# A row softmax on one core: the first load issued ahead of the entry barrier

## Chip, cores and metric

One NeuronCore of one Trainium2 chip. The metric is the device time of one execution in microseconds (us), as the median of a few runs.

## The reference

```python
x: (16, 1024, 512) float32
x_max = max(x, axis=-1)
exp_x = exp(x - x_max)
out   = exp_x / sum(exp_x, axis=-1)
```

It reads 33.55 MB and writes 33.55 MB.

## The kernel before

The 16384 rows are cut into 16 tiles of 128 partitions x 8 rows x 512 (2 MB each). Loads are issued by SyncE, stores by ScalarE. VectorE takes the row maxima and does the scaling, ScalarE the exponentials and their sums. The tiles have twelve buffers, and the loads run far ahead of the stores: in the packet records of this kernel the last load packet ends at 131.6 us, the last store packet at 160.17.

```python
CHUNKS = [8] * 16
SLOTS = {8: 12}
# ... pools, views src[k] and dst[k] ...
    def load(k):
        R = CHUNKS[k]
        tiles[k] = data.tile([P, R, d], F32, name=f"x{R}", tag=f"x{R}", bufs=SLOTS[R])
        nc.sync.dma_start(out=tiles[k], in_=src[k])
    # ... rowmax(k): one VectorE reduction of 128x4096
    # ... exps(k): 8 ScalarE activations with row sums
    # ... scale(k): one reciprocal and 8 multiplications on VectorE
    def store(k):
        nc.scalar.dma_start(out=dst[k], in_=tiles[k])

    with tc.manual_schedule():
        for k in range(K):
            load(k)
            rowmax(k)
            exps(k)
            if k >= 1:
                scale(k - 1)
                store(k - 1)
        scale(K - 1)
        store(K - 1)
```

What the source does not show is the program's first block, which the framework writes ahead of this code. Its instructions stand in the trace. GpSimd fills four small constants by memset, from 0.24 to 0.44 us. Then all five engines pass a barrier, a point that none leaves before all have reached it, kept by semaphores (counters that engines raise and wait for): each of the other four drains and adds one to a semaphore, between 0.01 and 0.34 us; GpSimd drains from 0.30 to 0.49, looks at that semaphore at 0.53, and at 0.61 releases them through a second one; they go on at 0.65 to 0.66. All code above stands behind that barrier, the first load too, which is issued at 0.73.

## Time and profile before

Time before: 163.15 us (162.96 to 163.39, 3 runs), span of the profiled run 161.3 us.

| what | us | where to read it |
|---|---|---|
| work of the 16 DMA engines | 158.2 of 161.3 | queue table: 49.5% + 48.6% of the span |
| VectorE busy | 123.8 | busy table |
| ScalarE busy | 93.2 | busy table |
| SyncE held by the entry barrier | 0.7 | waits of SyncE's queue |
| first load's issue starts | 0.73 | timeline |

The page's DMA lines of the kernel before follow; a packet is one of the pieces in which a DMA moves its data, of 16 KB in this kernel. The first two lines have 40 equal slices of the span, about 4 us each: the busy share of the DMA engines in tenths, and GB/s moved.

```profile
DMA  6999999999999999999999999999999999999993
GB/s 163 431 427 427 431 435 378 418 445 431 423 439 431 421 435 431 431 439 418 439 435 427 431 427 435 435 425 435 431 427 439 431 427 427 431 435 431 431 435 171
...
q1 hardware_dynamic: 2304, 33.56, 49.5%
q10 hardware_dynamic: 2304, 33.56, 48.6%
```

The reader should see a stream that is full from the second slice to the last but one. Queue 1 carries the loads and queue 10 the stores. Only the first and the last slice are short (163 and 171 GB/s; the others have 378 to 445), and from the first packet's start at 1.74 us to the last one's end at 160.17 there are 158.4 us for 158.2 us of work. So a change elsewhere can hardly win anything; time is to be had at the two ends alone.

Now the start. In the timeline (start, duration, engine; "SPq" is SyncE's queue issuing DMAs, merged over several issues) of the kernel before:

```profile
0.24 0.10 POOL L110 MEMSET const-float32-0.0<- 128x1 f32 x1 [0.24 <-issue]
...
0.33 0.10 POOL L110 MEMSET const-uint8-127<- 128x1 uint8 x1
0.73 8.22 SPq L52 DMA_DIRECT2D x<-in_x_dram  x7
8.64 4.42 DVE L57 TENSOR_REDUCE shift<-x 128x8 f32<-128x4096 f32 x1 [8.64 <-DMA x<-in_x_dram]
```

And in the waits of SyncE's queue (total us, times, longest), the line of the entry barrier:

```profile
SPq L110 <- PEq L110: 0.7, 1, 0.7
```

Nothing is loaded until SyncE is through the barrier, at 0.73 us, and nothing is computed until the first tile has landed, at 8.64 us. The wait line names PE, because TensorE was the last engine to add to the semaphore. But the records of the single instructions show that GpSimd was the last at the barrier: SyncE arrives at 0.00 us, VectorE and ScalarE at 0.13, TensorE at 0.32, and GpSimd looks at the count at 0.53, after its memsets and its drain, and releases at 0.61.

### The profile page before, as it was taken

What the parts mean: (1) busy time and instruction counts of PE and PEld (TensorE: products, weight loads), DVE (VectorE), ACT (ScalarE), POOL (GpSimd) and SP (SyncE); (2) the same over time, 40 slices, a digit from 0 to 9 for tenths busy, and PEclk for the clock granted to TensorE, in tenths of its full rate; (3) what the DMA queues carried; (4) which work ended last, traced back from release to release, by engine and by line L of the source; (5) the groups of instructions that cost most, each with busy time, mean ns of one, the idle gap of its engine ahead of it and who ended that gap; (6) DMA issues with size and microseconds to landing.
All of it is one profiled execution on the core that took longest, in us unless ns stands there. A gap on an engine that the chain in (4) does not pass through costs nothing.

```text
span 161.3 us, 527 instructions
## 1 busy us (share of the span) xinstructions
DVE 123.8 (77%) x160; ACT 93.2 (58%) x257; POOL 0.2 (0%) x4
## 2 busy tenths in 40 slices
DVE  0088799999999999985970079999999999957000
ACT  0037994959596867067002996859595959591000
POOL 0000000000000000000000000000000000000000
DMA  6999999999999999999999999999999999999993
GB/s 163 431 427 427 431 435 378 418 445 431 423 439 431 421 435 431 431 439 418 439 435 427 431 427 435 435 425 435 431 427 439 431 427 427 431 435 431 431 435 171
DMA packets 4612, 67.14 MB, mean 416 GB/s; under 512 B 513, under 2 KB 513, under 8 KB 513
## 3 DMA queue, kind: packets, MB, share of 16 engines
q1 hardware_dynamic: 2304, 33.56, 49.5%
q10 hardware_dynamic: 2304, 33.56, 48.6%
q14 instruction: 4, 0.02, 0.0%
HBM read 33.55 MB, written 33.55 MB: 416 GB/s over the span
## 4 chain that ended last, share of the span: by engine, by line
DMA 52%; DVE 31%; ACT 6%; SPq 2%; issue 1%; ACTq 1%; DVEq 0%
DMA x<-in_x_dram 52%; DVE shift L57 16%; DVE x L77 14%; ACT x L63 6%; SPq L52 2%; DVE recip L75 1%; ACTq L84 0%; DVEq L121 0%; ACTq L63 0%
## 5 line engine op out<-in xcount | busy, mean ns | idle before, releaser
L63 ACT ACTIVATE x<-x,shift 128x512 f32<-128x512 f32 x128 | 90.5, 709 | 44.1 <-DVE shift L57 21.4
L57 DVE TENSOR_REDUCE shift<-x 128x8 f32<-128x4096 f32 x16 | 70.6, 4415 | 9.7 <-DMA x<-in_x_dram 9.7
L77 DVE TENSOR_SCALAR x<-x,recip 128x512 f32<-128x512 f32 x128 | 52.1, 482 | 0.6
L63 ACT ACTIVATION_READ_ACCUMULATOR x<-x,shift 128x1 f32 x128 | 24.0, 187 | 0.0
L75 DVE RECIPROCAL recip<-sums 128x8 f32<-128x8 f32 x16 | 3.1, 196 | 15.3 <-ACT x L63 15.3
L63 ACT ACT_TABLE_LOAD x1 | 1.3, 1283 | 8.7 <-DMA x<-in_x_dram 8.7
L110 POOL MEMSET const-bfloat16-1.0<- 128x1 bf16 x1 | 0.1, 102 | 0.0
L110 POOL MEMSET const-uint8-127<- 128x1 uint8 x1 | 0.1, 102 | 0.0
L110 POOL MEMSET const-float32-0.0<- 128x1 f32 x1 | 0.1, 99 | 0.2 <-issue 0.2
L110 POOL MEMSET const-float32-1.0<- 128x1 f32 x1 | 0.1, 99 | 0.0
## 6 DMA issues: line engine op xcount, KB each, us to landing
x<-in_x_dram SPq DMA_DIRECT2D x16, 2048.0 KB, 42.6
out_dram<-x ACTq DMA_DIRECT2D x16, 2048.0 KB, 18.0
```

The lines of the kernel that those rows point to most:

```text
L52: nc.sync.dma_start(out=tiles[k], in_=src[k])
L57: nc.vector.reduce_max(out=shift[k], in_=tiles[k], axis=AX, negate=True)
L63: nc.scalar.activation(out=tiles[k][:, r, :], in_=tiles[k][:, r, :], func=EXP, bias=shift[k][:, r : r + 1], scale=1.0, accum_out=sums[k][: ...
L75: nc.vector.reciprocal(out=recip, in_=sums[k])
L77: nc.vector.tensor_scalar_mul(out=tiles[k][:, r, :], in0=tiles[k][:, r, :], scalar1=recip[:, r : r + 1],)
L110: nc = _bacc.Bacc("TRN2", target_bir_lowering=False, num_devices=1)
```

## The change

The intent: SyncE reaches the barrier first and idles there, from 0.00 to 0.65 us. The first load waits for nothing, since its buffer is fresh and its input is there, so it can be issued in that idle time. The edit works on the finished program: it takes the first DMA out of the kernel's block and puts it ahead of SyncE's drain in the first block.

```diff
+def first_load_at_the_head(nc):
+    main, body = nc.main_func.blocks[0], nc.main_func.blocks[1]
+    dmas = [i for i in body.instructions if type(i).__name__ == "InstDMACopy"]
+    load = dmas[0]
+    assert load.engine == mybir.EngineType.SP
+    body.instructions.remove(load)
+    barrier = next(
+        n
+        for n, i in enumerate(main.instructions)
+        if i.engine == mybir.EngineType.SP and type(i).__name__ == "InstDrain"
+    )
+    main.instructions.insert(barrier, load)
 # ...
     nc = tc.nc
+    nc.at_finalize(first_load_at_the_head)
```

## The prediction

> **What bounds it now.** The 16 DMA engines. The queue table gives loads 49.5% and stores 48.6% of their span: 98.1% of 161.3 us, or 158.2 us. In the slices DMA stands at 9 tenths in 38 of 40, near 430 GB/s; only the first (163 GB/s) and the last (171) are short. [...] In the packet records the first load packet starts at 1.74 us and the last store packet ends at 160.17: a window of 158.4 us for 158.2 us of work, so time can only be won at its two ends. The timeline has VectorE and ScalarE done at 149.5 us.
>
> **The start (instruction records).** SyncE reaches the barrier first, at 0.00 us. VectorE and ScalarE come at 0.13 to 0.14, TensorE at 0.32; GpSimd is last: its four memsets (0.24 to 0.44) and its drain (0.18 us) let it see all four at 0.53 and release at 0.61. SyncE is released at 0.65 and issues the first load at 0.73. The wait view of SyncE's queue shows the same: 0.7 us, once. First packet 1.01 us after the issue began, 0.64 after it ended; tile complete at 8.63.
>
> **What the change does.** It adds and removes no instruction and no byte. It moves one issue of 0.37 us ahead of SyncE's barrier wait, into idle time. Order on other engines is unchanged.
>
> - Gain: the first issue at about 0.00 instead of 0.73, the first packet at about 1.0.
> - Kept later? The second load issues right after the barrier, at 0.75 to 0.85 (1.15 before). The first 2 MB need 4.9 us at 430 GB/s, so the engines never run out. The whole stream should move up.
> - Cost: SyncE arrives at about 0.40 and drains. A drain does not wait for the data: ScalarE's after the last store's issue took 0.15 us while that store ran for 10 us more. So SyncE is through at about 0.57, near the 0.53 at which GpSimd looks; the barrier may slip 0.05 to 0.1 us. Nothing critical waits for it: later loads have 4 us of slack, the engines wait for data until about 8 us.
>
> **Critical path.** All of the 0.73 us, since the first load heads the DMA stream and the first reduction. I take 0.7, allowing for an issue slightly after SyncE's arrival. That is 0.4%. Measured time is 1.8 us over the span; I take that as fixed.
>
> **Predicted:** 163.15 - 0.7 = 162.45 us; 162.0 to 162.9 eight times in ten. Faster by over 2%: 0.01; within 2%: 0.97; slower by over 2%: 0.02.
>
> **What would show it.** First load issued near 0 us; second at 0.75 to 0.85; first packet near 1.0; first reduction at about 7.9 instead of 8.64; first slice up from 163 to about 240 GB/s (0.73 us at 430 is 0.31 MB, my estimate); span 160.6; DMA work still about 158 us; last compute 0.7 us earlier.
>
> **What would make it wrong.** SyncE's drain waiting for the load to land: every engine held to about 8 us, the DMA engines dry for about 2 us between loads one and two, and the time up by 1 to 3 us. A slow first issue so early, or something in the launch that holds its packets. A span that starts with SyncE, whose arrival need not be tied to the measured start of the run. The two streams meeting in another phase[...].

Two passages of this text are cut where marked: a sentence that set the rate of the full slices beside a figure from outside this case, and the size put on the last risk, which no run showed. The 430 GB/s used in the text is read from the GB/s line above.

## The result

| | median us | range | runs | span of the profiled run |
|---|---|---|---|---|
| before | 163.17 | 162.96 to 163.39 | 4 | 161.3 |
| after | 162.39 | 162.29 to 162.55 | 4 | 160.6 |

The ratio is 0.9953, with a 95% interval of 0.9936 to 0.997. Here and below a ratio is the mean time of one kernel's runs over that of the other's runs of the same rounds, so it is not quite the ratio of the medians quoted. The kernel is 0.78 us faster, well inside the 2% that counts as the same, yet clear of noise.

The DMA lines of the page after:

```profile
DMA  7999999999999999999999999999999999999993
GB/s 233 441 424 428 441 420 371 437 430 428 428 433 433 430 424 437 437 420 437 424 437 441 420 432 428 433 439 420 428 433 432 441 428 424 433 433 437 424 433 167
...
q1 hardware_dynamic: 2304, 33.56, 49.7%
q10 hardware_dynamic: 2304, 33.56, 48.8%
```

Only the first slice has clearly changed, from 163 to 233 GB/s; the others differ by at most 19 GB/s, either way. The shares have risen because the span is shorter: 98.5% of 160.6 us is 158.2 us of work, as before.

The timeline and the barrier's wait line after:

```profile
0.00 8.04 SPq L68 DMA_DIRECT2D x<-in_x_dram  x7
0.23 0.10 POOL L126 MEMSET const-float32-0.0<- 128x1 f32 x1 [0.23 <-issue]
...
0.33 0.10 POOL L126 MEMSET const-uint8-127<- 128x1 uint8 x1
7.72 4.42 DVE L73 TENSOR_REDUCE shift<-x 128x8 f32<-128x4096 f32 x1 [7.72 <-DMA x<-in_x_dram]
```

```profile
SPq L126 <- PEq L126: 0.2, 1, 0.2
```

The issue starts at 0.00, the first reduction 0.92 us earlier. The barrier itself opens a little later: GpSimd releases at 0.654 instead of 0.608 us, because SyncE's drain after the issue takes 0.13 us and ends at 0.55. The second load is issued at 0.78 us (1.15 before), and nothing else that waits at the barrier is needed so soon: the first reduction starts at 7.72.

To see whether the lead is kept I sorted the end times of all 4096 data packets (16 KB each) of each trace. This is a reading of the raw packet records:

| packet, in order of its end | before, us | after minus before, us |
|---|---|---|
| 16th | 3.76 | -0.78 |
| 128th | 8.04 | -0.78 |
| 512th | 22.62 | -0.78 |
| 1025th | 42.70 | -0.75 |
| 1537th | 62.15 | -0.64 |
| 3073rd | 120.56 | -0.66 |
| last | 160.17 | -0.69 |

The whole stream is moved, by the 0.73 us that the issue has moved, give or take 0.1.

### The profile page after: what moved, and what is told of

Same layout as the page of the kernel before. It is cut to its first block, busy times and chain, and to the rows that moved or that the text cites. A ratio compares the mean times of both kernels' runs of the same rounds, so it can differ in the third digit from the quotient of the medians. Undisturbed runs are those within 1.5% of the kernel's fastest.

```text
span 160.6 us, 527 instructions
## 1 busy us (share of the span) xinstructions
DVE 123.8 (77%) x160; ACT 93.2 (58%) x257; POOL 0.2 (0%) x4
## 4 chain that ended last, share of the span: by engine, by line
DMA 52%; DVE 31%; ACT 7%; SPq 1%; issue 1%; ACTq 0%; DVEq 0%
DMA x<-in_x_dram 52%; DVE shift L73 16%; DVE x L93 14%; ACT x L79 7%; SPq L68 1%; DVE recip L91 1%; ACTq L100 0%; DVEq L137 0%; ACTq L79 0%
```

## The experiments

The theory: the time is the moment at which the DMA stream starts, plus a fixed length, as long as the engines never run dry; the change moves that start. Rivals: the gain comes from compute starting earlier; or from the barrier or the later loads having moved; or the start is covered by slack and the gain has another source. All results were correct against the reference. "Before" is the kernel before on the same chip, in the same rounds. The changed kernel was not run again there: where a run is set against its 162.39 us, the two are of different rounds, in which the kernel before agrees (163.10 to 163.19, against 163.17).

| run | us (range) | before | ratio, 95% interval |
|---|---|---|---|
| 1: before, barrier 3.9 us later | 167.02 (166.91 to 167.24) | 163.13 | 1.0238, 1.0224 to 1.0251 |
| 2: after, barrier 3.9 us later | 163.64 (163.10 to 164.53) | 163.13 | 1.0032, 1.0009 to 1.0054 |
| 3: after, barrier 10 us later | 168.14 (168.07 to 168.36) | 163.13 | 1.0307, 1.0293 to 1.032 |
| 4: six loads ahead, barrier 10 us later | 162.29 (162.26 to 162.41) | 163.13 | 0.9948, 0.9936 to 0.996 |
| 5: two loads ahead, barrier 3.9 us later | 162.37 (162.18 to 162.47) | 163.10 | 0.9952, 0.9939 to 0.9964 |
| 6: one load ahead, barrier 1.9 us later | 162.43 (162.25 to 162.49) | 163.10 | 0.9954, 0.9941 to 0.9966 |
| 7: second load ahead instead of the first | 162.21 (162.16 to 162.48) | 163.10 | 0.9948, 0.9936 to 0.9961 |
| 8: first load in 64-partition halves, two queues | 168.03 (167.52 to 168.46) | 163.10 | 1.0293, 1.027 to 1.0316 |
| 9: first load in row halves, two queues | 162.41 (162.27 to 162.63) | 163.19 | 0.9954, 0.994 to 0.9967 |
| 10: 64-partition halves, one queue | 166.64 (166.46 to 166.84) | 163.19 | 1.0212, 1.0198 to 1.0226 |
| 11: row halves, one queue | 162.48 (162.42 to 162.74) | 163.19 | 0.9961, 0.9949 to 0.9974 |
| 12: before, without the four memsets | 155.00 (154.55 to 155.06) | 163.19 | 0.9493, 0.948 to 0.9506; not comparable, see 12 |

### 1. The barrier is made late, and the load stands behind it

GpSimd gets extra memsets of a scratch tile, moved into the first block ahead of its drain. They are about 1.0 us apart.

```diff
+    scratch = data.tile([P, PAD], F32, name="scratch", tag="scratch", bufs=1)   # PAD = 1024
     with tc.manual_schedule():
+        for _ in range(NPAD):                                                   # NPAD = 4
+            nc.gpsimd.memset(scratch, 0.0)
+    # on the finished program: these NPAD memsets to GpSimd's end of the barrier
```

> The kernel before, with four extra GpSimd memsets of 128x1024 ahead of the barrier, so that SyncE is released d later than 0.65 us (d is read from the trace; I guess 3 to 5 us). The first load still stands behind the barrier. Theory (the time hangs on when the first load is issued, and the DMA engines are full from then on): time = before + d, all of it, because the stream starts d later and nothing can be caught up. Rival (the start is hidden by slack somewhere later, and the 0.7 us of the change came from something else): clearly less than d is lost, down to nothing.

The timeline of this run:

```profile
0.37 3.98 POOL L118 MEMSET scratch<- 128x1024 f32 x4
4.66 3.15 SPq L81 DMA_DIRECT2D x<-in_x_dram  x6
```

The issue starts at 4.66 instead of 0.73 us, 3.93 later, and the time rises by 167.02 - 163.13 = 3.89 us. A delay of the first issue is paid in full and nowhere caught up. The rival with slack somewhere later falls.

### 2. The same late barrier, with the load ahead of it

```diff
+    # as in 1, NPAD = 4, and the first load to SyncE's end of the barrier
```

> The changed kernel with the same four extra memsets. Theory: the first load is issued at 0.0 us all the same, its 2 MB keep the DMA engines busy until about 7 us, the second load needs about 1 us from issue to first packet, so any barrier that opens before about 6 us costs nothing: time within 0.3 us of the changed kernel (162.4), although all engines are held d longer. If the barrier opens at 6 to 7 us, up to 1 us is lost. Rival (the change helped by opening the barrier or the rest of the program earlier): time = changed + d.

The time is 163.64 us: of the 3.9 us of delay, 1.25 us are lost against 162.39, and the runs scatter over 1.4 us. This was a miss for my "within 0.3 us". The load ahead of the barrier saves most of the 3.9 us, though not all, so the rival "changed + d" (166.3) falls too. The windows of 1 us around the place where the first load runs out (the last two columns are the DMA share and GB/s) show this, here the changed kernel:

```profile
7.00:8.00 1.00, 0.28 (x1) 0.23 (x1) 0.00 (x0) 1.00 1.07 459
8.00:9.00 1.00, 1.00 (x1) 1.00 (x1) 0.00 (x0) 1.00 0.99 426
```

and here this run:

```profile
7.00:8.00 1.00, 0.12 (x1) 0.07 (x1) 0.00 (x0) 1.00 0.92 328
8.00:9.00 1.00, 1.00 (x1) 1.00 (x1) 0.00 (x0) 1.00 0.85 360
```

Between 7 and 9 us the stream is short of its 430 GB/s. In the packet records the packets that end there took 0.70 and 0.66 us on average, up to 1.0, instead of 0.61. Runs 5 and 6 below ask whether the late second load is the reason.

### 3. A barrier so late that the first load is used up

```diff
+    # as in 2, NPAD = 10
```

> The changed kernel with ten extra memsets: the barrier opens at r (about 8 to 12 us), when the first load has been consumed. Theory: the engines run dry from about 7.3 us until r + 1.1 us (second load's issue to first packet), so time = 162.4 + (r + 1.1 - 7.3), give or take 0.6 us for ramps; the packet records show one gap of that length. Rival (only the first load's place matters): 162.4.

SyncE is released at 10.62 us, so the expectation was 162.4 + (10.62 + 1.1 - 7.3) = 166.8, give or take 0.6. Measured: 168.14. The direction is right, but the size is 1.3 us short, outside the margin of 0.6. The windows show why:

```profile
6.00:7.00 1.00, 0.00 (x0) 0.00 (x0) 0.94 (x2) 1.00 0.65 279
7.00:8.00 1.00, 0.00 (x0) 0.00 (x0) 0.94 (x2) 1.00 0.04 16
8.00:9.00 1.00, 0.00 (x0) 0.00 (x0) 0.94 (x2) 1.00 0.00 0
...
11.00:12.00 1.00, 1.00 (x1) 1.00 (x1) 0.00 (x0) 1.00 1.08 213
12.00:13.00 1.00, 1.00 (x1) 0.05 (x1) 0.00 (x0) 1.00 0.45 131
13.00:14.00 1.00, 1.00 (x1) 0.00 (x0) 0.00 (x0) 1.00 0.86 360
```

The engines do run dry: the first load's last packets end between 6.8 and 7.7 us, and the next packet starts at 11.66. (A packet's bytes and time are shown where it starts, so 11 to 12 us shows packets that had only begun.) Then they need until about 14 us to be back at rate: the first sixteen packets again take 0.6 to 1.8 us each, most of them over 1 us, as at the program's start (0.95 to 1.86 us in the kernel before, where later ones take 0.61). My sum left out this second ramp (the time that a starting stream needs to come to its full rate). From the packet records, the 256th packet is 5.65 us later than in the changed kernel: 4.4 us of this are the gap of my sum, the rest is the ramp.

### 4. The same very late barrier, six loads ahead of it

```diff
+    # NPAD = 10, and the first six loads to SyncE's end of the barrier
```

> As the run with ten memsets, but with all six loads that wait for nothing placed ahead of the barrier (12 MB, 29 us of stream). Theory: the DMA engines never run dry, and compute, which starts at r instead of 7.7 us, has some 10 us of slack at the end, so the time is back within 0.5 us of 162.4. Rival (the loss of the ten-memset run is the late compute, not the dry engines): as slow as that run.

162.29 us: everything is back. Two lines of its timeline:

```profile
2.71 10.25 SPq L81 DMA_DIRECT2D x<-in_x_dram  x3
10.74 4.42 DVE L86 TENSOR_REDUCE shift<-x 128x8 f32<-128x4096 f32 x1 [10.74 <-PEq L142]
```

The first reduction starts at 10.74 us, just as late as in run 3, and is held by the barrier; the time does not care. What run 3 lost was the dry stream, not the late compute.

### 5 and 6. Why run 2 lost 1.25 us

```diff
+    # 5: NPAD = 4, two loads ahead of the barrier
+    # 6: NPAD = 2, one load ahead of the barrier
```

> The four-memset run took 163.64 us, 1.25 more than I expected, with a wide spread (163.1 to 164.5). Theory A (partly dry engines): the second load, issued at 4.66 us, reached the engines too late to be queued behind the first load's last packets, which shows as packets of 0.7 us mean instead of 0.61 between 7 and 9 us. Here the same four memsets stand ahead of the barrier, but two loads stand ahead of it too. A: back at 162.4, within 0.25, spread back to 0.3 us. Theory B (the memsets themselves, or the late barrier, cost it): as slow as that run, 163.6.

> One load ahead of the barrier, two extra memsets, so the barrier opens at about 2.6 us and the second load is issued at about 2.7, 4 us before the first load's last packets. Theory A: 162.4, within 0.25, although the barrier is 2 us later than in the changed kernel. Theory B: about half of the loss of the four-memset run, 163.0.

162.37 and 162.43 us, both with the small spread back. Run 5 has the same memsets and the same late barrier as run 2, so neither of these cost anything. Its windows at the place where run 2 fell short:

```profile
7.00:8.00 1.00, 0.28 (x1) 0.24 (x1) 0.00 (x0) 1.00 0.96 410
8.00:9.00 1.00, 1.00 (x1) 1.00 (x1) 0.00 (x0) 1.00 1.07 459
```

With the second load issued at 2.64 us (run 6) nothing is lost; at 4.66 (run 2) 1.25 us are. So the latest harmless issue of the second load lies somewhere between 2.6 and 4.7 us, although the first load's last packets end only around 7 us. Run 6 also rules out that the change won its time by issuing the second load earlier (0.78 us against 1.15 before): here it is issued later than before, and the time is the changed kernel's. In the packet records run 2 is 0.48 us behind the changed kernel at the 256th packet, 0.8 at the 769th, about where the stores begin, and 1.07 at the last.

The order of packet ends hides one thing that the landing marks of the same two traces show. Each DMA leaves 16 marks as its parts land. For the second load their mean is only 0.37 us later in run 2, but the last of them comes at 14.00 us instead of 12.59, and 0.96 us after the one before it. The third and fourth loads show the same gap and again end 1.4 us late (18.90 against 17.48, 23.80 against 22.37), and the last mark of the last store is 1.09 us late (160.90 against 159.81). So in this one trace the loss is there from the second load on, at first chiefly in one part of sixteen, and compute starts only after the last mark (the first reduction at 7.88 us, the first load's last mark at 7.85). By the last store the mean of the marks is 0.82 us late too. The marks do not tell which engine the slow part belongs to. Why it fell behind, how the lag spread, and why the loss scatters from run to run, is open.

### 7. The second load ahead of the barrier instead of the first

```diff
-    # dmas[0] is moved
+    # dmas[1] is moved: tile 1 lands first, tile 0 after it
```

> The second load, not the first, is placed ahead of the barrier; the first stays behind it. The stream starts at the same time as in the changed kernel, but tile 0 lands about 5 us later, so the first reduction starts at about 12.6 us instead of 7.7. Theory (what counts is when the DMA stream starts): 162.4, within 0.3. Rival (what counts is when the first tile is ready for compute): no gain over the kernel before, rather a loss of some 4 us (167).

The timeline of this run:

```profile
12.63 4.42 DVE L84 TENSOR_REDUCE shift<-x 128x8 f32<-128x4096 f32 x1 [12.63 <-DMA x<-in_x_dram]
```

The first reduction starts 4.9 us later than in the changed kernel and even 4 us later than before, and the time is 162.21 us, the changed kernel's within noise. So the earlier compute that the change brings is worth nothing here. What counts is when the stream starts, with any load.

### 8 to 11. Can the ramp be shortened as well?

In the changed kernel the first packet starts at 1.02 us and the 16th ends at 2.99; at full rate the 16 engines would have a packet each by 1.63 (an estimate: 1.02 plus the 0.61 us of a steady packet). I tried to shorten this by having two queues issue halves of the first load.

```diff
-        nc.sync.dma_start(out=tiles[k], in_=src[k])
+        if k == 0:                        # 8
+            h = P // 2
+            nc.sync.dma_start(out=tiles[k][:h], in_=src[k][:h])
+            nc.scalar.dma_start(out=tiles[k][h:], in_=src[k][h:])
+        else:
+            nc.sync.dma_start(out=tiles[k], in_=src[k])
+    # 9: halves [:, :h] and [:, h:] with h = R // 2; 10: as 8, both by sync; 11: as 9, both by sync
+    # in all four both halves go ahead of the barrier
```

> The first load is cut in two halves of 64 partitions, one issued by SyncE and one by ScalarE, both ahead of the barrier[...]. In the changed kernel the first packet starts at 1.02 us and the 16th ends at 2.98 (a full-rate start would have it end at 1.63). If the issue time of 0.37 us is part of that ramp, the 64th packet ends 0.1 to 0.25 us earlier than in the changed kernel and the time is 162.15 to 162.3[...]. Half the chance each.

> The first load cut in two again, one half by SyncE and one by ScalarE ahead of the barrier, but each half of all 128 partitions (4 of their 8 rows, packets of 8 KB). The run with 64-partition halves took 5 us more (I had expected 0 to 0.25 less): its packets took 1.29 us instead of 0.61. Theory S[...]: here no such packets, time 162.2 to 162.6. Theory Q (two queues at once in the first microseconds disturb each other): several us slower, 165 or more. The first question stays too: is the 64th packet's worth of bytes (1.05 MB) earlier than in the changed kernel (4.82 us)?

> Both 64-partition halves issued by SyncE, one after the other, ahead of the barrier. Theory S: the halves run at about 200 GB/s one after the other, some 5 us lost: 167 to 168.5, packets of 1.2 to 1.3 us until about 11 us. Theory Q: full rate, 162.4.

> The control of the two-queue run by rows: the same two halves of 128 partitions, both issued by SyncE ahead of the barrier. Packets of 8 KB. Time 162.4 within 0.25; if the smaller first packets shorten the ramp, 1 MB is in before 4.82 us and the time is 162.2. The difference to the two-queue run is the second queue's alone.

Three clauses are cut from these texts, since no run shows the mechanisms that they name: one from run 8's reason for two queues, one from its other case (no gain, 162.4 us, which had the other half of the chance), and the reason given for theory S. Theory S, and what runs 9 and 10 test, is that the cut by partitions makes the packets slow. Its about 200 GB/s in run 10's text are an estimate from run 8: a packet of 16384 bytes in 1.29 us on each of 16 engines makes 203.

Run 8 was a bad miss: 168.03 us. Its two possible causes, the 64 partitions and the second queue, are told apart by 9 and 10. With two queues but all 128 partitions (9) nothing is lost; with one queue and 64 partitions (10) 3.5 us are lost against before. The start of run 10's GB/s line:

```profile
GB/s 191 191 254 429 401 441 445 425 401 443 445 429 421 421 443 441 425 413 437 445 433 417 421 445 437 429 415 433 441 441 429 413 433 441 437 417 421 445 441 147
```

In the second slice the halves move at 191 GB/s, under half of the 441 that the 128-partition loads reach in that slice of the changed kernel. Run 11, with the same one queue and two halves but all 128 partitions, takes 162.48 us, so it is the cut by partitions that costs; why it does was not shown. I had not thought of it when I cut the load that way. Run 8 lost 1.4 us more than run 10: its second half, issued by ScalarE at 0.12 us, had its first packet only at 5.9 us (in run 9, issued at the same time, at 2.80). Why it was held is open.

The ramp question itself: in runs 9 and 11, with packets of 8 KB, the first 1.05 MB are in at 4.41 and 4.46 us instead of 4.86, and the first 8.4 MB at 21.70 and 21.68 instead of 21.89. But 33 MB are in at 79.72 and 79.83 instead of 79.63. I take a part of the early lead to be only that small packets are counted as done sooner, which no run shows; the 0.2 us that is left is gone again after the stores have begun. With 162.41 and 162.48 us there is no gain, and two queues do no better than one. The ramp stays, and what makes it was not shown.

### 12. A shorter barrier in the kernel before

```diff
+    # the kernel before; the four InstMemset of the first block are removed (nothing reads them)
```

> The kernel before, first load behind the barrier, with GpSimd's four unused constant memsets removed, so that GpSimd is no longer late. TensorE then comes last (0.32 us), so the first load's issue should move from 0.73 to 0.55 to 0.65 us, and the time by the same 0.1 to 0.2 us: 162.95 to 163.05 if before is 163.1; the stream's lead in the packet records is the same 0.1 to 0.2. If the barrier's length is not what the change hid, no such lead.

The measured time is 155.00 us (154.55 to 155.06), which looks like 8.2 us won. It is not. The head of the page and the timeline of this run:

```profile
span 161.0 us, 523 instructions
```

```profile
0.56 8.21 SPq L59 DMA_DIRECT2D x<-in_x_dram  x7
8.45 4.42 DVE L64 TENSOR_REDUCE shift<-x 128x8 f32<-128x4096 f32 x1 [8.45 <-DMA x<-in_x_dram]
```

The span is 161.0 us, 0.3 less than before. In all other runs the measured time is 1.73 to 1.84 us above the span; here it is 6.1 to 6.5 us below. The numbers fit a measured time that begins at the first instruction run by an engine itself, not by its sequencer. In the kernel before that is the first memset, at 0.24 us. From there to the end of the span it is 161.3 - 0.24 = 161.06 us, and that profiled run measured 163.08, which is 2.02 us more. Here the first such instruction is the reduction at 8.45 us, and 161.0 - 8.45 + 2.02 = 154.57, where the profiled run measured 154.55. In all 14 profiled runs the measured time is 2.01 to 2.03 us more than the stretch from that first instruction to the end; but only this run moves that instruction by more than 0.01 us, so the reading rests on one contrast. By it, the run only took the start of the clock away, and its measured time cannot be set against the others.

By the trace the expectation held: the issue starts at 0.56 instead of 0.73 us, 0.17 earlier, so the four memsets account for 0.17 of the 0.65 us for which the barrier held SyncE; and the spans of the four runs have a median of 161.2 us against 161.4 of the kernel before on the same chip. The lead in the packet records is 0.18 us at the start of the first packet, 0.06 at the end of the 16th, 0.18 at the 3841st and 0.32 at the last, so single traces give a lead only to about 0.1 us.

## Why the prediction was right

- **What bounds the kernel.** Right. 158.2 us of DMA work before and after, and no slice but the first changed clearly. Single slices stand at up to 445 GB/s, since the page counts a packet's bytes in the slice where it starts; with each packet's bytes spread over its own time no slice of either trace is above 432, and a steady packet of 16384 bytes in 0.611 us on each of 16 engines makes 429.
- **What moves, and by how much.** Right: the issue from 0.73 to 0.00 us, the first packet from 1.74 to 1.02, the second load at 0.78 (foretold 0.75 to 0.85), the barrier 0.046 us later (0.05 to 0.1), the first slice at 233 GB/s (240), the span at 160.6 (160.6).
- **That all of it counts and is kept.** Right: 0.78 us of 0.73, within noise; 162.39 against 162.45. Runs 1 and 3 show that a later start or a gap is paid in full, and run 7 that the first reduction plays no part. There the prediction said that the first load "heads the DMA stream and the first reduction"; the second half of this is true and worth nothing.
- **That the drain does not wait for the data.** Right: SyncE's drain took 0.13 us while the load ran until 7.7 us.
- **The 1.8 us above the span as fixed.** Right for the change, whose first memset stays at 0.23 us. Run 12 shows that it is not a constant of the launch. The prediction named a risk of this kind (a measured start not tied to the span's) without testing it; that the change leaves the first memset where it was is luck in this respect.
- **Where it was off.** "Later loads have 4 us of slack" was an estimate, and run 2 shows less, as a second load 3.9 us later costs 1.25 us. It did not matter, since the change moves the second load the other way. The first tile landed 0.92 us earlier instead of 0.73, and the last store was issued 0.49 us earlier (149.49 to 148.99) instead of 0.7; neither is on the path that sets the time.

Nothing beats the changed kernel clearly. Run 7 (162.21) and run 4 (162.29) are its equals within noise.

## What to carry to other kernels

This was shown on one kernel. Where the DMA engines are full from first to last, as here, the time is the start of the stream plus its length. So move the first transfer that waits for nothing as early as the program allows, never mind whether the first compute gains, and expect just the microseconds by which its issue moves (here 0.78 us for 0.73). Make sure that more transfers are queued well before the first is used up: here a dry stream cost its gap and a new ramp of about 1.3 us (run 3), and a second load issued too late, at 4.66 us, cost 1.25 us though the stream never stopped (run 2), where one at 2.64 us cost nothing (run 6). And read the span beside the measured time whenever an edit touches the first instruction of a program, because the clock may start at it.
